# A hybrid attention trunk on one core: tiles of SBUF moved to multiples of 1 and 2 KB

## The chip, the core and the metric

The program runs on one core of a Trainium2 chip, as one launch. The metric is the device time of one execution in microseconds (us); the median of three executions stands for a kernel.

A core has five engines with their own instruction streams: TensorE (PE; the loads of its stationary operand are listed apart, as PEld), VectorE (DVE), ScalarE (ACT), GpSimd (POOL) and SyncE (SP, which here issues all DMA). They share SBUF, 128 partitions of on-chip memory. A tile takes the same bytes of each partition, so its place is one number, its offset in bytes from the start of a partition.

## What is computed

One decoder layer on x of 2048 rows by 1024 columns, in float32, then a last normalization. Cut to what matters:

```python
h = rmsnorm(x, norm_attn)
proj = h @ w_in                              # 1024 x 2700
o_A = stick_breaking(...)                    # 4 heads, all earlier keys
o_B = native_sparse(...)                     # compressed, selected and window branches
o_C = differential(...)                      # 4 heads, two softmax maps each
o_D = sliding_window(...)                    # window 128, sinks
x = x + (concat(norm(o_A), norm(o_B), o_C, norm(o_D)) * g_mix) @ w_out
u = relu(rmsnorm(x, norm_mlp) @ w_up)        # 1024 x 4096
x = x + (u * u) @ w_down                     # 4096 x 1024
return rmsnorm(x, norm_final)
```

## The kernel before

**Stages.** The rows are worked in four chunks of 512. Stages P0 to P3 project a chunk (w_in), stages M0 to M3 do for a chunk what follows the attention: w_out, w_up, w_down and the last normalization. The attention of groups A, C, D and B (loops over 128 queries) runs between them and beside them. A planner in Python, with costs per instruction, decides while the program is written which stream gives PE its next matmul; dense matmuls fill in where a score or value matmul would have to wait. The order on each engine is fixed then. M3 is the last stage, and all attention is over when it runs.

**Dense matmuls in three products.** A float32 operand is split into a rounded part (hi) and the rest (lo), both of type fp32r, and a product is hi*hi + lo*hi + hi*lo, summed in PSUM. PE streams one operand (moving, up to 512 columns) past another (stationary, 128 columns). In a row of the profile, `pdM<-T_hi,w_lo` has the moving operand first and the stationary one second.

- The normalized chunk lies transposed in `T_hi` and `T_lo` (128 x 8 x 512). For w_up and most of w_in it is the moving operand, 512 columns wide, with 128 columns of `w_hi` or `w_lo` stationary (lines 529 and 606).
- For w_down the weight is the moving operand, 512 columns wide, and `u_hi` or `u_lo` (the squared activations) is stationary (line 647).
- For w_out and the value columns of w_in the weight moves, 256 or 268 columns wide, and T is stationary (lines 556 and 591). At the start of each w_up stage T moves in halves of 256 columns (line 634).
- Scores move a key tile `kst`, up to 512 columns (lines 988, 1092).

**The way of a weight.** `load_weights` (line 366) issues the DMA of 512 KB into one of two `raw` tiles; `split_weights` (line 380) writes `w_hi` on ACT and `w_lo` on DVE or POOL into one of three pairs, and gives `raw` back; `weights` (line 398) hands the pair to the matmuls. The order of the weights is that of `weight_specs` (line 325).

**The last normalization.** In the last step of each M stage, for each of four blocks of 128 rows, DVE multiplies by the root mean square and by `last_gain` (lines 657 to 665), and SP stores the rows. `last_gain` is a tile of its own, 4 KB of each partition, loaded once when M0 is written (line 576).

**Where tiles lie.** A pool's tiles follow one another in the order in which they are first made, each place rounded up to 32 bytes; pools stand in the order const, at, dn. The first 16,512 bytes are the program's own. Offsets in bytes, and what is left when they are divided by 1024 and by 128:

| tile | offset of the first buffer | mod 1024 | mod 128 |
|---|---|---|---|
| ident (const) | 16,512 | 128 | 0 |
| row, qst, kst, v, PT, oS, on, scr (at) | row 34,496, kst 71,360 | 704 | 64 |
| small tiles of the attention and pc (at) | 118,464 to 124,063 | any | any |
| T_hi, T_lo, acc, nx (dn) | 124,064 / 140,448 / 156,832 / 173,216 | 160 | 32 |
| small tiles of the norms (dn) | 181,408 to 181,631 | any | any |
| raw, w_hi, w_lo, u_lo, u_hi, r (dn) | 181,632 / 189,824 / 202,112 / 214,400 / 220,544 / 226,688 | 384 | 0 |

Buffers of these tiles are 1, 2, 4, 8 or 16 KB, so every buffer of a tile has the same remainder by 1024. The last tile ends at 228,736 of 229,376 bytes.

Of the kernel before, what the change touches and what calls it, by code (L numbers as in the profile page):

```python
# [9 lines left out]
F32 = mybir.dt.float32  # L10
F32R = mybir.dt.float32r
# [8 lines left out]
D = 1024  # L20
# [11 lines left out]
QB, RB, PB, WB = 4, 7, 3, 3  # L32
PD, ZB, TB = 3, 2, 2
GROUPS = "ACDB"
OFF = S - 128
UO = 2 * (NT - 1)
UW = UO + 32
# [29 lines left out]
def dap(t, off, dims):  # L67
    return bass.AP(tensor=t.tensor, offset=t.offset + off, ap=dims)
# [128 lines left out]
class Trunk:  # L197
# [4 lines left out]
    def __init__(self, ctx, tc, args):  # L202
        self.tc, self.nc = tc, tc.nc
        self.__dict__.update(args)
        nc = self.nc
        self.plan = Plan()
        self.A = Engine(self.plan, "A", nc.scalar, cost_act)
        self.V = Engine(self.plan, "V", nc.vector, cost_dve)
        self.G = Engine(self.plan, "G", nc.gpsimd, cost_pool)
        self.const = ctx.enter_context(tc.tile_pool(name="const", bufs=1))  # L210
        self.dram = ctx.enter_context(tc.tile_pool(name="scratch", bufs=1, space=DRAM))
        self.psum = ctx.enter_context(tc.tile_pool(name="psum", bufs=1, space=PSUM))
        self.at = ctx.enter_context(tc.tile_pool(name="at", bufs=1))
        self.dn = ctx.enter_context(tc.tile_pool(name="dn", bufs=1))
        self.T = (self.dn.tile([128, KD, 512], F32R, name="T_hi", bufs=1),
                  self.dn.tile([128, KD, 512], F32R, name="T_lo", bufs=1))
        self.Tw, self.Tr = [0.0] * 4, [0.0] * 4
        self.filled, self.used, self.fill = [0] * 4, [0] * 4, 0
        self.source, self.added, self.gain = [], {}, {}
        nc.scalar.preload_act_table_set("natural_log_exp_and_others")  # L220
        self.res = {"row": Res(RB), "kst": Res(3), "v": Res(2), "qst": Res(QB), "PT": Res(PB), "w": Res(WB),
                    "raw": Res(2), "nx": Res(2), "acc": Res(4), "oS": Res(3), "pc": Res(1), "unit": Res(UNITS)}
        self.constants()
        self.scratch()
        self.rawq, self.wq = [], []
        self.mix_n = [0] * NT
        self.stored = {}
        self.vq, self.fq = [], []
        self.kq = {}
        self.over, self.pa = set(), "A0"  # L230
        self.compress_due = self.compressed = 0


    def tile(self, pool, shape, dt, name, bufs, tag=None):
        t = pool.tile(shape, dt, name=name, tag=tag or name, bufs=bufs)
        self.plan.new(tag or name, bufs, t.tensor.name)
        return t
# [61 lines left out]

    def constants(self):  # L300
        V, G, const = self.V, self.G, self.const
        self.ident = const.tile([128, 128], F32, name="ident")
        G.memset(self.ident, 1.0)
        G.affine_select(self.ident, self.ident, [[-1, 128]], OP.is_equal, 0.0, base=0, channel_multiplier=1)
        self.mhalf = const.tile([128, 1], F32, name="mhalf")
        G.memset(self.mhalf, -0.5)
        self.qsc = const.tile([128, 6], F32, name="qsc")
        self.qs_col = {}
        for j in range(2):
            for n, (g, sl, dd) in enumerate((("B", SL_NSA, 64), ("C", SL_DIFF, 32), ("D", SL_SWA, 64))):  # L310
                col = n * 2 + j
                self.qs_col[f"q{g}{j}"] = col
                for hh in range(2):
                    V.memset(self.qsc[64 * hh:64 * hh + 64, col:col + 1], -(dd ** -0.5) / sl[2 * j + hh])
# [10 lines left out]
    def weight_specs(self):  # L325
        def w_in(cols, k0, kn):
            wd = sum(w for _, w in cols)
            parts, o = [], 0
            for c0, w in cols:
                def place(t, o=o, w=w):  # L330
                    return t[:, :kn * wd].rearrange("p (k w) -> p k w", k=kn)[:, :, o:o + w]

                parts.append((place, dap(self.w_in, k0 * 128 * IN_COLS + c0,
                                         [[IN_COLS, 128], [128 * IN_COLS, kn], [1, w]])))
                o += w
            return parts

        def up(ft):
            return [(lambda t: t.rearrange("p (k w) -> p k w", k=KD),
                     dap(self.w_up, ft * 128, [[FF, 128], [128 * FF, KD], [1, 128]]))]  # L340

        for kind, c in self.phases:
            if kind == "P":
                for m in ORDER[c > 0]:
                    if m in MT:
                        yield kind, c, w_in(MT[m], 0, KD)
                    else:
                        kn = WMAX // sum(w for _, w in NG[m])
                        for k0 in range(0, KD, kn):
                            yield kind, c, w_in(NG[m], k0, min(kn, KD - k0))  # L350
            else:
                for d in range(4):
                    for kk in range(2):
                        yield kind, c, [(lambda t: t.rearrange("p (k w) -> p k w", k=4),
                                         dap(self.w_out, kk * 512 * D + d * 256, [[D, 128], [128 * D, 4], [1, 256]]))]
                yield kind, c, up(0)
                yield kind, c, up(1)
                for fc in range(FF // 128 // FC):
                    if FC * fc + 2 < FF // 128:
                        yield kind, c, up(FC * fc + 2)  # L360
                    for f in range(FC):
                        yield kind, c, [(lambda t: t, dap(self.w_down, (fc * FC + f) * 128 * D, [[D, 128], [1, D]]))]
                    if FC * fc + 3 < FF // 128:
                        yield kind, c, up(FC * fc + 3)

    def load_weights(self):
        for kind, c, parts in self.weight_specs():
# [12 lines left out]
    def split_weights(self):  # L380
        j = 0
        while True:
            while not self.rawq:
                if "raw" in self.over:
                    return
                yield None
            yield from self.res["w"].take()
            kind, c, raw, n = self.rawq.pop(0)
            hi = self.tile(self.dn, [128, WMAX], F32R, "w_hi", WB)
# [179 lines left out]
    def mlp(self, c):  # L569
# [2 lines left out]
        self.ph = f"M{c}"  # L572
        V, A = self.V, self.A
        acc = []
        if c == 0:
            self.last_gain = self.const.tile([128, D], F32, name="last_gain")
            self.ld(self.last_gain, dap(self.norm_final, 0, [[0, 128], [1, D]]))
        yield from self.res["acc"].take(4)
        for i in range(4):
            a = self.acc_tile()  # L580
# [56 lines left out]
        for fc in range(FF // 128 // FC):  # L637
# [4 lines left out]
            for i in range(4):  # L642
# [14 lines left out]
                if last:  # L657
                    V.tensor_tensor(ss[:, 0:1], ss[:, 0:1], ss[:, 1:2], OP.add)
                    r = self.rstd(dn, ss[:, 0:1], D, "nt")
                    for d in range(2):  # L660
                        o = acc[i][:, d * 512:d * 512 + 512]
                        V.scalar_tensor_tensor(o, o, r[:, 0:1], self.last_gain[:, d * 512:d * 512 + 512], op0=OP.mult,
                                               op1=OP.mult)
                        self.st(dap(self.out, (c * 512 + i * 128) * D + d * 512, [[D, 128], [1, 512]]), o)
                    self.res["acc"].give()
            if FC * fc + 3 < FF // 128:
                yield from up(FC * fc + 3)
            if fc == FF // 128 // FC - 2:
# [6 lines left out]
    def attention_constants(self):  # L675
# [21 lines left out]
        G.affine_select(mask, mask, [[-1, 128]], OP.is_gt, -BIG, base=0, channel_multiplier=1)  # L697
        self.maskr = const.tile([128, 128], F32R, name="maskr")
        V.tensor_copy(self.maskr, mask)
        self.identr = const.tile([128, 128], F32R, name="identr")  # L700
        V.tensor_copy(self.identr, self.ident)

        self.neglam = const.tile([128, 1], F32, name="neglam")
        dl = []
        for a_, b_, nm in ((self.diff_lq1, self.diff_lk1, "l1"), (self.diff_lq2, self.diff_lk2, "l2")):
            u = self.row_tile()[:, :64].rearrange("p (a b) -> p a b", a=2)
            self.ld(u[:, 0, :], dap(a_, 0, [[0, 128], [1, 32]]))
            self.ld(u[:, 1, :], dap(b_, 0, [[0, 128], [1, 32]]))
            s_ = const.tile([128, 1], F32, name="lams_" + nm)
            V.tensor_tensor_reduce(u[:, 0, :], u[:, 0, :], u[:, 1, :], 1.0, 0.0, OP.mult, OP.add, s_)  # L710
            A.activation(s_, s_, AF.Exp)
            dl.append(s_)
        V.tensor_tensor(self.neglam, dl[1], dl[0], OP.subtract)
        V.tensor_scalar(self.neglam, self.neglam, -LAM_INIT, None, op0=OP.add)

        self.snk = const.tile([128, 4], F32, name="snk")
        self.ld(self.snk, dap(self.sinks, 0, [[0, 128], [1, 4]]))
        self.nsnk = const.tile([128, 4], F32, name="nsnk")
        V.tensor_scalar(self.nsnk, self.snk, -1.0, None, op0=OP.mult)

        self.kcs = const.tile([128, 128], F32R, name="kcs")
# [846 lines left out]
```

## Time and profile before

| | us |
|---|---|
| median of three executions | 3219.77 |
| lowest and highest of them | 3219.07, 3225.04 |
| the profiled execution, its own time | 3224.61 |
| its span, first to last instruction | 3222.9 |

The profile is of one execution, and its durations belong to the 3224.61 us. A matmul's listed duration (about 0.39 us at 512 columns) holds its way through the array; the next one starts before it ends. What a stream of matmuls costs is therefore the step from one start to the next, which the timeline shows to 0.01 us; over 25 steps it is known to better than 1 ns.

### The profile page before, as it was taken

The numbers are of one execution on the slowest core, as the hardware profiler recorded it, in microseconds if no ns is written. First come the engines' busy times: TensorE is split into PE (matmuls) and PEld (weight loads), VectorE is DVE, ScalarE is ACT, GpSimd is POOL, SyncE is SP. The second block draws the span as 40 slices with busy tenths as digits, with TensorE's granted clock in tenths as the row PEclk, the third lists the DMA queues.
The fourth block names the chain that finished last, engine by engine and source line by source line (L and its number), as shares of the span: only waits on it lengthen the run. The fifth ranks groups of instructions, "written<-read, shape, count | busy, mean of one in ns | idle before, by whom it ended". The sixth has DMA issues, their size and how long they took to land.

```text
span 3222.9 us, 51242 instructions
## 1 busy us (share of the span) xinstructions
PE 3128.8 (97%) x19152; PEld 2510.3 (78%) x19152; DVE 2063.7 (64%) x4278; ACT 1776.0 (55%) x3459; POOL 714.2 (22%) x479
## 2 busy tenths in 40 slices
PE   7999999999999999999999999999999999999998
PEld 6887877878877777778877677778777777888886
DVE  4774668645668877666658887777655554545545
ACT  4764667545667755555657775565555543333333
POOL 3042312323212122232211122233212112310000
PEclk9999999999999999999999999999999999999999
DMA  7777555664133343364232333444522222423332
GB/s 213 193 193 206 160 160 148 191 176 134 57 97 87 100 110 105 97 164 121 61 100 68 99 95 88 110 117 134 141 63 83 65 61 74 149 81 97 92 98 85
DMA packets 456649, 376.53 MB, mean 117 GB/s; under 512 B 127056, under 2 KB 405712, under 8 KB 454736
## 3 DMA queue, kind: packets, MB, share of 16 engines
q1 hardware_dynamic: 456400, 373.26, 42.0%
q8 instruction: 151, 2.47, 0.3%
q14 instruction: 98, 0.80, 0.1%
HBM read 319.59 MB, written 53.58 MB: 116 GB/s over the span
## 4 chain that ended last, share of the span: by engine, by line
PE 77%; DVE 9%; ACT 5%; DMA 4%; issue 2%; SPq 1%; POOL 1%; DVEq 0%; POOLq 0%; ACTq 0%
PE pdM L290 43%; PE pdP L290 11%; DVE row L116 7%; PE tB L294 4%; PE oB L290 4%; PE zB L290 4%; ACT row L116 4%; PE oC L290 2%; PE zC L290 2%; PE tC L294 2%; SPq L246 1%; PE oA L290 1%; DVE acc L116 1%; PE tA L294 1%; PE zA L290 1%
## 5 line engine op out<-in xcount | busy, mean ns | idle before, releaser
L116 POOL TENSOR_TENSOR w_lo<-raw,w_hi 128x1024 fp32r<-128x1024 f32 (+1 forms) x188 | 469.4, 2501 | 1248.9 <-ACT w_hi L116 1105.4
L116 ACT ACTIVATE w_hi<-raw 128x1024 fp32r<-128x1024 f32 (+2 forms) x376 | 388.2, 1047 | 499.4 <-PE pdM L290 309.5
L116 DVE TENSOR_TENSOR acc<-acc,pdM 128x512 f32<-128x512 f32 (+1 forms) x576 | 370.3, 654 | 193.5 <-PE pdM L290 182.0
L290 PE MATMUL pdM<-T_lo,w_hi 128*128 128x512 f32 (+1 forms) x1088 | 419.6, 386 | 4.4 <-POOL T_lo L116 4.4
L290 PE MATMUL pdM<-T_hi,w_hi 128*128 128x512 f32 (+1 forms) x1088 | 419.5, 387 | 3.8 <-DVE nx L116 2.2
L290 PE MATMUL pdM<-T_hi,w_lo 128*128 128x512 f32 (+1 forms) x1088 | 420.8, 387 | 0.0
L290 PE MATMUL pdM<-w_hi,u_hi 128*128 128x512 f32 x1024 | 405.5, 403 | 11.6 <-DVE acc L116 8.4
L290 PE MATMUL pdM<-w_hi,u_lo 128*128 128x512 f32 x1024 | 405.2, 396 | 3.9 <-DVE u_lo L116 3.9
L290 PE MATMUL pdM<-w_lo,u_hi 128*128 128x512 f32 x1024 | 404.7, 396 | 0.0
L116 DVE TENSOR_TENSOR w_lo<-raw,w_hi 128x1024 fp32r<-128x1024 f32 (+1 forms) x188 | 241.2, 1290 | 214.5 <-ACT w_hi L116 206.0
L116 ACT ACTIVATE row<-row 128x1024 f32<-128x1024 f32 (+7 forms) x292 | 229.0, 801 | 118.5 <-DVE row L116 115.8
L290 PEld LDWEIGHTS pdM<-T_lo,w_hi 128*128 128x128 f32 x1088 | 206.5, 190 | 45.9 <-POOL T_lo L116 4.9
L290 PEld LDWEIGHTS pdM<-T_hi,w_hi 128*128 128x128 f32 x1088 | 206.0, 190 | 45.3 <-DVE nx L116 2.5
L116 ACT ACTIVATE PT<-tB 128x512 f32<-128x512 f32 (+1 forms) x260 | 135.9, 532 | 189.4 <-PE tB L294 186.7
L290 PEld LDWEIGHTS pdM<-T_hi,w_lo 128*128 128x128 f32 x1088 | 206.4, 190 | 42.1 <-issue 1.0
L290 PEld LDWEIGHTS pdM<-w_hi,u_hi 128*128 128x128 f32 x1024 | 193.2, 189 | 58.0 <-DVE acc L116 13.2
L290 PEld LDWEIGHTS pdM<-w_hi,u_lo 128*128 128x128 f32 x1024 | 193.7, 189 | 42.7 <-DVE u_lo L116 5.3
L290 PEld LDWEIGHTS pdM<-w_lo,u_hi 128*128 128x128 f32 x1024 | 193.6, 189 | 41.4 <-issue 1.2
L116 ACT ACTIVATE row<-row,c_mn 128x1024 f32<-128x1024 f32 (+4 forms) x192 | 171.6, 896 | 85.6 <-DVE c_mn L116 84.4
L290 PE MATMUL pdP<-T_hi,w_lo 128*128 128x512 f32 x480 | 194.1, 404 | 3.7 <-DVE w_lo L116 3.7
L290 PE MATMUL pdP<-T_lo,w_hi 128*128 128x512 f32 x480 | 193.4, 403 | 0.0
L290 PE MATMUL pdP<-T_hi,w_hi 128*128 128x512 f32 x480 | 192.7, 401 | 0.0
(209 smaller groups left out, 6604.8 us busy)
## 6 DMA issues: line engine op xcount, KB each, us to landing
raw<-in_w_up_dram SPq DMA_DIRECT2D x128, 512.0 KB, 4.1
raw<-in_w_down_dram SPq DMA_DIRECT2D x128, 512.0 KB, 3.6
raw<-in_w_in_dram SPq DMA_DIRECT2D x72, 512.0 KB, 4.9
acc<-in_x_dram SPq DMA_DIRECT2D x32, 512.0 KB, 4.3
raw<-in_w_out_dram SPq DMA_DIRECT2D x32, 512.0 KB, 4.4
qst<-qk_qA SPq DMA_DIRECT2D x64, 128.0 KB, 3.5
qst<-qk_qC SPq DMA_DIRECT2D x128, 64.0 KB, 2.6
qst<-qk_qD SPq DMA_DIRECT2D x64, 128.0 KB, 3.4
```

The source lines that it names most:

```text
L116: return f(*a, **k)
L246: self.nc.sync.dma_start(dst, src)
L290: self.nc.tensor.matmul(out, a, b, start=start, stop=stop, **k)
L294: self.nc.tensor.transpose(out, a, self.ident[:a.shape[0], :a.shape[0]])
```

## The change

Five edits. (1) A tile `pad` of 816 floats is made first in the pool const. (2) A pool `sm` is opened ahead of at and dn, and takes every tile of theirs whose elements per partition are no multiple of 256. (3) `last_gain` is gone: each M stage ends its list of weights with norm_final, which is loaded into a `raw` tile, handed on unsplit, and given back after the fourth block of rows. (4) `ident` is gone: the identity is built in a row tile, copied to `identr`, and `ident` is `identr` read as float32. (5) Two pairs of small constants share a tile.

```diff
+PAD = 816
...
+        self.sm = ctx.enter_context(tc.tile_pool(name="sm", bufs=1))
         self.at = ctx.enter_context(tc.tile_pool(name="at", bufs=1))
...
+        self.const.tile([128, PAD], F32, name="pad")
         self.constants()
...
     def tile(self, pool, shape, dt, name, bufs, tag=None):
+
+        if pool in (self.at, self.dn) and math.prod(shape[1:]) % 256:
+            pool = self.sm
...
-        self.ident = const.tile([128, 128], F32, name="ident")
-        G.memset(self.ident, 1.0)
-        G.affine_select(self.ident, self.ident, [[-1, 128]], OP.is_equal, 0.0, base=0, channel_multiplier=1)
+        one = self.row_tile()[:, :128]
+        G.memset(one, 1.0)
+        G.affine_select(one, one, [[-1, 128]], OP.is_equal, 0.0, base=0, channel_multiplier=1)
+        self.identr = const.tile([128, 128], F32R, name="identr")
+        V.tensor_copy(self.identr, one)
+        self.ident = self.identr.bitcast(F32)
...
                     if FC * fc + 3 < FF // 128:
                         yield kind, c, up(FC * fc + 3)
+                yield "G", c, [(lambda t: t, dap(self.norm_final, 0, [[0, 128], [1, D]]))]
...
+            if self.rawq[0][0] == "G":
+                self.wq.append(self.rawq.pop(0)[2])
+                continue
             yield from self.res["w"].take()
...
-        if c == 0:
-            self.last_gain = self.const.tile([128, D], F32, name="last_gain")
-            self.ld(self.last_gain, dap(self.norm_final, 0, [[0, 128], [1, D]]))
...
+                    if i == 0:
+                        gain, = yield from self.weights()
                     for d in range(2):
                         o = acc[i][:, d * 512:d * 512 + 512]
-                        V.scalar_tensor_tensor(o, o, r[:, 0:1], self.last_gain[:, d * 512:d * 512 + 512], op0=OP.mult,
+                        V.scalar_tensor_tensor(o, o, r[:, 0:1], gain[:, d * 512:d * 512 + 512], op0=OP.mult,
                                                op1=OP.mult)
                         self.st(dap(self.out, (c * 512 + i * 128) * D + d * 512, [[D, 128], [1, 512]]), o)
                     self.res["acc"].give()
+                    if i == 3:
+                        self.res["raw"].give()
...
-        dl = []
-        for a_, b_, nm in ((self.diff_lq1, self.diff_lk1, "l1"), (self.diff_lq2, self.diff_lk2, "l2")):
+        lams = const.tile([128, 2], F32, name="lams")
+        dl = [lams[:, 0:1], lams[:, 1:2]]
+        for a_, b_, s_ in ((self.diff_lq1, self.diff_lk1, dl[0]), (self.diff_lq2, self.diff_lk2, dl[1])):
...
-        self.snk = const.tile([128, 4], F32, name="snk")
+        snk = const.tile([128, 8], F32, name="snk")
+        self.snk, self.nsnk = snk[:, 0:4], snk[:, 4:8]
```

## Rows read from the trace of the kernel before

**Rows 1.** The page: busy time and instructions of each engine; the chain by engine.
```profile
PE 3128.8 (97%) x19152; PEld 2510.3 (78%) x19152; DVE 2063.7 (64%) x4278; ACT 1776.0 (55%) x3459; POOL 714.2 (22%) x479
...
PE 77%; DVE 9%; ACT 5%; DMA 4%; issue 2%; SPq 1%; POOL 1%; DVEq 0%; POOLq 0%; ACTq 0%
```

**Rows 2.** Windows: stretch, length, busy of PE, PEld, DVE, ACT, POOL; clock, DMA.
```profile
1700.00:2000.00 300.00, 287.40 (x1695) 216.20 (x1692) 245.28 (x316) 215.38 (x340) 56.62 (x26) 0.98 0.32 86
...
2900.00:3180.00 280.00, 280.00 (x1217) 227.99 (x1216) 143.33 (x180) 94.92 (x124) 0.00 (x0) 1.00 0.32 96
```

**Rows 3.** The chain in order of time, 2700 to 3223 us: start, length, what.
```profile
2863.62 345.87 PE pdM L290 x1523
```

**Rows 4.** Groups of instructions on PE, by form: count, busy us, mean ns.
```profile
L290 PE MATMUL pdM<-w_hi,u_hi 128*128 128x512 f32 x1024 | 405.5, 403 | 11.6 <-DVE acc L116 8.4 <-ACT u_hi L116 2.3 <-ACT r L116 0.8
...
L290 PE MATMUL pdM<-T_hi,w_lo 128*128 128x512 f32 x960 | 383.0, 399 | 0.0
...
L290 PE MATMUL pdP<-T_hi,w_lo 128*128 128x512 f32 x480 | 194.1, 404 | 3.7 <-DVE w_lo L116 3.7
...
L290 PE MATMUL pdM<-w_hi,T_hi 128*128 128x256 f32 x512 | 145.9, 287 | 0.0
...
L290 PE MATMUL zB<-kst,qst 128*128 128x512 f32 x328 | 106.6, 416 | 0.8 <-DVE b_mw L116 0.7
```

**Rows 5.** Timeline of PE in M3, w_up: first and last of 26.
```profile
3172.94 0.40 PE L290 MATMUL pdM<-T_hi,w_hi 128*128 128x512 f32 x1
...
3178.77 0.40 PE L290 MATMUL pdM<-T_lo,w_hi 128*128 128x512 f32 x1
```

**Rows 6.** Timeline of PE in M3, w_down: first and last of 27.
```profile
3188.94 0.39 PE L290 MATMUL pdM<-w_hi,u_hi 128*128 128x512 f32 x1
...
3194.83 0.39 PE L290 MATMUL pdM<-w_lo,u_hi 128*128 128x512 f32 x1
```

**Rows 7.** Timeline of PE in M3, w_out, 256 columns: first and last of 10.
```profile
2809.83 0.28 PE L290 MATMUL pdM<-w_hi,T_lo 128*128 128x256 f32 x1
...
2810.89 0.28 PE L290 MATMUL pdM<-w_hi,T_lo 128*128 128x256 f32 x1
```

**Rows 8.** Timeline of PE in M3, w_up in halves: first and last of 11.
```profile
2864.78 0.28 PE L290 MATMUL pdM<-T_lo,w_hi 128*128 128x256 f32 x1
...
2865.94 0.28 PE L290 MATMUL pdM<-T_hi,w_lo 128*128 128x256 f32 x1
```

**Rows 9.** Timeline of PE, eight transposes in one piece.
```profile
2794.39 1.03 PE L294 MATMUL pdM<-ident,nx 128*128 128x128 f32 x8
```

**Rows 10.** The tile ident: durations in ns, least, median, most.
```profile
L294 PE MATMUL pdM<-ident,nx x256: 270/273/477, 728.4 to 2859.4; 128*128 128x128 f32 x128
```

**Rows 11.** Groups of instructions on ACT, by form: count, busy us, mean ns.
```profile
L116 ACT ACTIVATE w_hi<-raw 128x1024 fp32r<-128x1024 f32 x364 | 378.6, 1055 | 495.2 <-PE pdM L290 309.5 <-DMA raw<-in_w_down_dram 72.0 <-issue 37.0
...
L116 ACT ACTIVATE nx<-acc 128x1024 f32<-128x1024 f32 x32 | 33.8, 1055 | 26.2 <-DMA acc<-in_x_dram 17.7 <-DVE acc L116 6.0 <-POOL T_lo L116 2.3
```

**Rows 12.** The tile last_gain: its DMA, from issue to landing.
```profile
DMA to landing us min/median/max: 7.0/7.0/7.0
```

**Rows 13.** Timeline of DVE where M2 ends and M3 has begun.
```profile
2807.22 1.41 DVE L116 SCALAR_TENSOR_TENSOR acc<-acc,nt_rs,last_gain 128x512 f32<-128x512 f32 x2 [0.20 <-POOL nt_rs L116]
...
2810.53 1.23 DVE L116 TENSOR_TENSOR w_lo<-raw,w_hi 128x1024 fp32r<-128x1024 f32 x1 [1.57 <-ACT w_hi L116]
```

**Rows 14.** The page's DMA issues: count, KB each, us to landing.
```profile
raw<-in_w_out_dram SPq DMA_DIRECT2D x32, 512.0 KB, 4.4
```

**Rows 15.** Timeline of DVE at the end of M3.
```profile
3195.86 2.35 DVE L116 TENSOR_TENSOR w_lo<-raw,w_hi 128x1024 fp32r<-128x1024 f32 x2
...
3213.10 1.40 DVE L116 SCALAR_TENSOR_TENSOR acc<-acc,nt_rs,last_gain 128x512 f32<-128x512 f32 x2
```

**Rows 16.** Timeline of all engines at the start.
```profile
2.41 0.56 DVE L116 CAST identr<-ident 128x128 fp32r<-128x128 f32 x1
...
11.34 1.97 PE L294 MATMUL pdP<-ident,acc 128*128 128x128 f32 x8 [11.34 <-DVE nt_ms L116]
```

More of the change, by code (lines that the diff above doesn't have):

```diff
@@ L699, in attention_constants @@
         V.tensor_copy(self.maskr, mask)
-        self.identr = const.tile([128, 128], F32R, name="identr")
-        V.tensor_copy(self.identr, self.ident)
         self.neglam = const.tile([128, 1], F32, name="neglam")
-        dl = []
-        for a_, b_, nm in ((self.diff_lq1, self.diff_lk1, "l1"), (self.diff_lq2, self.diff_lk2, "l2")):
+        lams = const.tile([128, 2], F32, name="lams")
+        dl = [lams[:, 0:1], lams[:, 1:2]]
+        for a_, b_, s_ in ((self.diff_lq1, self.diff_lk1, dl[0]), (self.diff_lq2, self.diff_lk2, dl[1])):
             u = self.row_tile()[:, :64].rearrange("p (a b) -> p a b", a=2)
@@ L708, in attention_constants @@
             self.ld(u[:, 1, :], dap(b_, 0, [[0, 128], [1, 32]]))
-            s_ = const.tile([128, 1], F32, name="lams_" + nm)
             V.tensor_tensor_reduce(u[:, 0, :], u[:, 0, :], u[:, 1, :], 1.0, 0.0, OP.mult, OP.add, s_)
             A.activation(s_, s_, AF.Exp)
-            dl.append(s_)
         V.tensor_tensor(self.neglam, dl[1], dl[0], OP.subtract)
         V.tensor_scalar(self.neglam, self.neglam, -LAM_INIT, None, op0=OP.add)
-        self.snk = const.tile([128, 4], F32, name="snk")
+        snk = const.tile([128, 8], F32, name="snk")
+        self.snk, self.nsnk = snk[:, 0:4], snk[:, 4:8]
         self.ld(self.snk, dap(self.sinks, 0, [[0, 128], [1, 4]]))
-        self.nsnk = const.tile([128, 4], F32, name="nsnk")
         V.tensor_scalar(self.nsnk, self.snk, -1.0, None, op0=OP.mult)
```

## The prediction

> **What bounds the kernel now.** I read the page first. PE is busy for 3128.8 of 3222.9 us and holds 77% of the chain that ended last [rows 1], so PE bounds the kernel unless it is busy only because its matmuls are listed long. The windows settle that: from 2900 to 3180 us PE is never idle, at a granted clock of 1.00 (the 2.4 GHz level), and starts 1217 matmuls in 280 us; from 1700 to 2000, in the attention, it is idle for 4% while DVE is busy for 82% [rows 2]. The chain by time says the same of M3: 345.87 us of it, to 11 us before the end, are one unbroken piece of PE [rows 3]. So a nanosecond off the step of a dense matmul shortens the kernel, and the next question is what sets that step.
>
> The timeline gives it. In w_up, where T moves, 25 steps take 5.83 us: 233.2 ns each [rows 5]. In w_down, where w moves, 26 steps take 5.89 us: 226.5 ns [rows 6]. Both move 512 columns of the same type past 128 fresh stationary columns, at the same clock; 512 columns at 2.4 GHz are 213.3 ns. So T's stream loses 19.9 ns and w's 13.2. The difference, 6.7 ns, is the time of 16 columns, or 64 bytes of a partition. What else separates them is where they lie: T's slices start 32 bytes past a multiple of 128, w's on a multiple of 128, both off any multiple of 256. The trace doesn't prove that this is the cause, but the layout is what this change alters.
>
> **The change part by part.**
>
> *The offsets after.* Const starts at 16,512 bytes, gains 3,264 for pad and loses 4,096 (last_gain), 512 (ident) and two places of 32 bytes: it ends at 33,088. The pool sm then takes 5,600 bytes of small attention tiles and 224 of small norm tiles: 38,912, which is 19 times 2,048. From there come only tiles of whole kilobytes. T_hi lands at 122,880, raw at 180,224, w_hi at 188,416, u_lo at 212,992, all multiples of 2,048; only oS, on and scr are at multiples of 1,024. It fits: r ends at 227,328.
>
> *T as the moving operand.* 3 x 960 matmuls in the M stages and 3 x 480 in the P stages, 4320 in all ([rows 4], where one of each three equal groups stands). Bounds: no gain at all, or down to the bare 213.3 ns, 4320 x 19.9 = 86 us. Between ends so far apart I take the nearest row: after the change T starts on a multiple of 128, as w does today, so it gets w's step: 4320 x 6.7 = 28.8 us.
>
> *w as the moving operand, 512 wide.* 3 x 1024 = 3072 matmuls [rows 4]. w already starts on a multiple of 128 and goes to one of 2,048. No operand of the trace lies so, and nothing says what the 13.2 ns are. Bounds: a gain of 3072 x 13.2 = 40.6 us; a loss if the common offset hurts, by the only loss the trace shows, 6.7 ns: 20.5 us. I take 0, as for T: no nearer row than w itself.
>
> *The 256-wide matmuls.* w moving past a stationary T steps at 1.06 / 9 = 117.8 ns [rows 7]; T moving past w at 1.16 / 10 = 116.0 [rows 8]; the columns alone need 106.7. Here the operand 32 bytes off is no slower, which speaks against the address (see the rivals). 3 x 512 and 3 x 256 matmuls: 0 taken, at most 2304 x 11.1 = 25.6 us. The scores move kst from a multiple of 64, and no long run of them stands in the trace: 0 to 5 us (776 x 6.7; 328 of them in rows 4), 0 taken.
>
> The rule of the Trainium skill that speaks against the change stands in "TensorE: Matmul & The Clock Gate", section "Back-to-back issue gap": a warm matmul follows the one ahead after its columns at 2.4 GHz plus about 2.5 ns, with no term for an address. By it both steps would be an estimated 215.8 ns and moving T would be worth 0 instead of 28.8 us. The trace disagrees with it on the step, 233.2 and 226.5 ns.
>
> *The other engines.* ACT takes 1055 ns for 1024 elements both from raw (a multiple of 128) and from acc (32 off) [rows 11]. So I give ACT and DVE nothing for their offsets. No row shows a DMA into a tile on a multiple of 256 bytes; whatever it gained could come only out of PE's idle time, 3222.9 - 3128.8 = 94 us in all and mostly not DMA's [rows 1], so I take 0.
>
> *norm_final through raw.* One DMA early in the program goes, four come, one at the end of each M stage, and each holds one of two raw tiles until the stage's last multiplication by the gain. At the end of M3 it is hidden: its raw tile is free when the last weights are split, at 3195.86 + 2.35 = 3198.2, a gain lands 7.0 us after its issue [rows 12], at 3205.2, and the first product with it starts at 3213.10 [rows 15]. That cover is 7.9 us; beyond it each us late is a us at the end, because DVE closes the kernel. At the three other ends the next stage's w_out tiles come through one raw tile meanwhile. At the end of M2 the third w_out tile can be loaded only when the second is split, and the fourth only when the last gain product is done, at 2807.22 + 1.41 = 2808.6; with 4.4 us to land [rows 14], 1.06 on ACT and 1.23 on DVE it is ready at 2815.3, against 2811.8 now [rows 13]. PE reaches it after the 96 matmuls of the first quarter, some 2 us sooner. SP's queue keeps behind that load the loads of acc, which are not wanted before; in DVE's queue nothing waits that hadn't. At M0 and M1 attention fills such gaps. Bounds: 0, and three times the whole way 4.4 + 1.06 + 1.23, 20 us. I take 3 us.
>
> *ident from identr.* A copy of 0.56 us that ran anyway now stands ahead of the first transpose. It ended at 2.97 us and PE starts at 11.34 [rows 16]: hidden by 8 us of normalizing; without that cover it would cost its 0.56 us. Merged constants, pad and sm issue nothing.
>
> *The sum.* Not all of the 28.8 us arrives: in the attention PE already waits for 4% [rows 2], and a faster PE waits more on DVE. I pass on nine tenths: 26 us, less 3 for raw, 23 us. The profiled execution would take 3224.6 - 23 = 3201.6; it lies 4.8 us above the median shown, so the median comes to 3219.8 - 23 = 3197 us. I call 0.2%, 6.4 us, the least that a measurement tells from no change; the three runs before spread over 6.0.
>
> **The rivals.**
>
> *All of the loss goes.* If a stream loses whatever a start off 1 or 2 KB costs, T and w both end near their columns. The nearest row for what then remains is the transposes: eight take 1.03 us, the last of them 0.27 [rows 9, 10], so the step is 0.76 / 7 = 108.6 ns, 1.9 above the 106.7 of the 256 columns that the planner counts. At 215.2 ns T gains 18.0 x 4320 = 77.8 us, w 11.3 x 3072 = 34.7, and the 256-wide ones at 108.6 gain 9.2 x 2304 = 21.2: 133.7, nine tenths 120, less 3: 3103 us. With every bound in full, 3219.8 - 86 - 40.6 - 25.6 = 3068. For it: w's offset isn't a multiple of 256 either, so w's 13.2 ns may be the rest of the same loss. Against: they may as well be the price of exchanging the stationary operand each time, which no address touches.
>
> *The address isn't it.* T and w differ also in who is stationary and in what came before. For it: at 256 columns T moves no slower than w [rows 7, 8]. Then the steps stay 233.2 and 226.5 and only raw is left: 3223 us, at worst 3240. The skill's rule, quoted above, would have this too.
>
> *One common offset hurts.* After the change every slice that moves and every slice loaded beside it starts at the same remainder of 512. If the two reads then meet in the same place of SBUF, w's step rises to T's of today, 3072 x 6.7 = 20.5 us, and T's stays: 3240 us, slower. It decides as soon as the mean step in M3's dense stretch is above today's 280 / 1217 = 230.1 ns [rows 2]. Against: u and w, both 384 past a multiple of 1,024 today, are the faster pair.
>
> **How the numbers follow.** Forecast 0.45, all of the loss 0.25, not the address 0.18, common offset 0.12. The forecast's own range, from two thirds of T's gain with 8 us lost at raw to all of it with kst's, is 3187 to 3209. The range for 8 in 10 leaves out the common offset and half of the no-change case, and takes the other case down to half-way between its price and its bound: 3085 to 3223. Faster by over 0.2%: the forecast and all of the loss, 0.70. Within 0.2%: most of not the address, 0.15. Slower: the common offset and the worst of raw, 0.15.
>
> **What would show it.** In M3's w_up the step of T: 226.5 right, 233.2 the address isn't it, near 215 all of the loss. In w_down the step of w: 226.5 right. At the end of M2, w_lo of the fourth w_out tile some 3 us later after M2's last gain product than now, and PE idle for at most a few us. In M3's tail no DVE wait on the gain. I am wrong if w's step moves, in either direction, or if T's steps fall and the attention stretches grow by as much.

## The result: 0.6% faster, for a cause that the forecast had half

The changed kernel takes 3202.74 us, the median of six runs (3196.0 to 3204.39), against 3219.7 for the kernel before beside it (six runs, 3217.99 to 3225.04): a ratio of 0.9939, 95% interval 0.9926 to 0.9952. On another chip it was 0.9933 (0.9919 to 0.9946). So it is faster by 17 to 21 us; the forecast was 23.

The profiled executions differ by more, 3224.61 and 3198.36 us, and the clock is part of that. By the trace's record of the granted clock, the execution of before ran 58.0 us at 1.2 GHz, apart from its tail, in 11 stretches, and this one 34.1 us in 7; the difference is worth up to 12 us. The second profiled execution of the changed kernel, with 47.8 us at that level, took 3206.63. Verdicts below go by medians and ratios, and the traces serve for steps and waits.

The page of the changed kernel answers [rows 1], PE's busy time first, then the chain by engine:

```profile
PE 3104.2 (97%) x19152; PEld 2510.6 (79%) x19152; DVE 2054.8 (64%) x4278; ACT 1777.8 (56%) x3459; POOL 714.6 (22%) x479
...
PE 75%; DVE 10%; ACT 7%; DMA 4%; issue 3%; SPq 1%; POOL 1%; DVEq 0%; POOLq 0%; ACTq 0%
```

The windows of the same stages, M3 shifted by its 21 us, answer [rows 2]: 1237 matmuls in 280 us of dense work in place of 1217, 226.4 ns each and not 230.1.

```profile
1700.00:2000.00 300.00, 284.23 (x1668) 214.95 (x1667) 242.45 (x321) 207.23 (x329) 59.86 (x26) 0.99 0.31 85
2879.00:3159.00 280.00, 280.00 (x1237) 231.86 (x1236) 145.01 (x181) 96.48 (x127) 0.00 (x0) 1.00 0.33 98
```

The chain by time answers [rows 3]: the same 1523 matmuls without a break take 5.25 us less. In the timeline of PE, T's step in w_up is (3153.44 - 3147.78) / 25 = 226.4 ns, where it was 233.2 [rows 5]; w's in w_down is 5.89 / 26 = 226.5, as before [rows 6].

```profile
2843.15 340.62 PE pdM L296 x1523
```

```profile
3147.78 0.39 PE L296 MATMUL pdM<-T_hi,w_hi 128*128 128x512 f32 x1
...
3153.44 0.39 PE L296 MATMUL pdM<-T_lo,w_hi 128*128 128x512 f32 x1
...
3162.74 0.39 PE L296 MATMUL pdM<-w_hi,u_hi 128*128 128x512 f32 x1
...
3168.63 0.39 PE L296 MATMUL pdM<-w_lo,u_hi 128*128 128x512 f32 x1
```

At 256 columns both streams became slower, which no part of the sum had. Nine steps in w_out take 1.08 us, 120.0 ns each, against 117.8 [rows 7]; ten in w_up's halves take 1.19 us, 119.0 against 116.0 [rows 8].

```profile
2788.42 0.28 PE L296 MATMUL pdM<-w_hi,T_lo 128*128 128x256 f32 x1
...
2789.50 0.28 PE L296 MATMUL pdM<-w_hi,T_hi 128*128 128x256 f32 x1
...
2843.49 0.28 PE L296 MATMUL pdM<-T_hi,w_hi 128*128 128x256 f32 x1
...
2844.68 0.28 PE L296 MATMUL pdM<-T_lo,w_hi 128*128 128x256 f32 x1
```

Over all long runs of one kind in the two traces, from start to start: T at 512 columns 233.3 and 227.4 ns, w at 512 227.8 and 227.4, w past T at 256 118.2 and 119.7, T past w at 256 116.8 and 119.5.

These are steps of long runs, and two thirds of T's 512-wide matmuls stand among the first ten of their run, ahead of the next matmul of another kind. There the gain is smaller. Mean step of T at 512 columns by its place in the run:

| step of the run | before, ns | after, ns |
|---|---|---|
| second to fourth | 232.4 | 230.5 |
| fifth to tenth | 233.3 | 228.1 |
| from the eleventh | 233.3 | 226.7 |

The means leave out steps over 0.3 us and those at 1.2 GHz. One run of seven, as an example: its six steps take 1.40 us before and 1.39 after.

```profile
1200.70 0.39 PE L290 MATMUL pdM<-T_hi,w_lo 128*128 128x512 f32 x1
...
1202.10 0.39 PE L290 MATMUL pdM<-T_hi,w_lo 128*128 128x512 f32 x1
```

```profile
1192.15 0.39 PE L296 MATMUL pdM<-T_hi,w_lo 128*128 128x512 f32 x1
...
1193.54 0.39 PE L296 MATMUL pdM<-T_hi,w_lo 128*128 128x512 f32 x1
```

Over all 4320 of them, from each start to the next, with waits over 0.15 us left out and time at 1.2 GHz counted half, they take 1031.1 us before and 1012.2 after: 4.4 ns less each, 18.9 us.

norm_final's raw tile did what was described, and PE hardly felt it. At the end of M2 the last gain product ends at 2786.61 + 1.42 = 2788.0, and w_lo of the fourth w_out tile at 2797.68 + 1.22 = 2798.9, 10.9 us later. Before it was 4.5 us (w_lo at 2811.95 to 2813.2 after 2808.6; the row of [rows 13] that I took for the fourth tile's is the third's). PE's waits from there to the first w_up tiles sum to 5.4 us, against 5.9 before, and none is for a weight. In all of M0 to M3 PE's waits for a weight sum to 0 us here, 2.2 in the second trace of this kernel and 0.2 before. At the end of M3, SP issues the gain's load at 3171.59, such loads land after 3.8 us, and the first product that needs it starts at 3187.38 without a wait: the cover is 12 us, not 7.9 [rows 12, 15]. DVE in its order of time:

```profile
2786.61 1.42 DVE L117 SCALAR_TENSOR_TENSOR acc<-acc,nt_rs,raw 128x512 f32<-128x512 f32 x2 [0.73 <-POOL nt_rs L117]
...
2797.68 1.22 DVE L117 TENSOR_TENSOR w_lo<-raw,w_hi 128x1024 fp32r<-128x1024 f32 x1 [0.19 <-ACT w_hi L117]
...
3187.38 1.40 DVE L117 SCALAR_TENSOR_TENSOR acc<-acc,nt_rs,raw 128x512 f32<-128x512 f32 x2
```

### The profile page after: what moved, and what is told of

The parts are those of the page before. It is cut to its first block, busy times and chain, and to the rows that moved or that the text cites. A ratio compares the mean times of both kernels' runs of the same rounds, so it can differ in the third digit from the quotient of the medians.

```text
span 3196.6 us, 51283 instructions
## 1 busy us (share of the span) xinstructions
PE 3104.2 (97%) x19152; PEld 2510.6 (79%) x19152; DVE 2054.8 (64%) x4278; ACT 1777.8 (56%) x3459; POOL 714.6 (22%) x479
## 4 chain that ended last, share of the span: by engine, by line
PE 75%; DVE 10%; ACT 7%; DMA 4%; issue 3%; SPq 1%; POOL 1%; DVEq 0%; POOLq 0%; ACTq 0%
PE pdM L296 41%; PE pdP L296 12%; DVE row L117 7%; ACT row L117 4%; PE tB L300 4%; PE oB L296 4%; PE zB L296 4%; PE oC L296 2%; PE zC L296 2%; PE tC L300 2%; SPq L252 1%; DVE acc L117 1%; ACT w_hi L117 1%; DMA raw<-in_w_in_dram 1%; PE oA L296 1%
```

## Experiments

Theory A, the forecast's: a moving slice that starts off a multiple of 128 bytes loses some 6 ns in 512 columns. Against it stood that tiles must lie at multiples of 1 or 2 KB (D), that the two operands' starts act together (B), and that the gain comes from the order of work or from norm_final (C). The first runs put E in A's place: the step goes by the difference of the two starts. The later ones added F: where a tile starts sets the cost of a DMA into it.

### Streams of matmuls (e1, e5)

```
for (w, m, s): 32 x (24 x in e5)  matmul(z[:, :w], st[:, s/4 + 128*(j%8):+128], mv[:, m/4 + 512*(j%8):+w])
```

> This kernel leaves the whole computation out: it runs streams of 32 dependent-free matmuls of constant data, each stream with one width (512 or 256 columns), one start of the moving slice and one start of the stationary slice in a partition's bytes, with a fresh stationary slice for each matmul or the same one throughout, and writes zeros and sums of constants to the output. Theory A (the start of the moving slice within 128 bytes sets the step): at 512 columns 227 ns for starts at 0, 128, 256, 384 and 512, 233 ns for 16, 32, 48, 96 and 160 bytes past a multiple of 2 KB, 64 undecided; the start of the stationary slice changes nothing. Rival B (the stationary slice's start, or the two together, set it): 227 ns for all moving starts, a change where the stationary one moves. Rival C (neither; what separated the two streams before was their content or their neighbours in time): 227 ns throughout. For 256 columns the two kernels' traces give 116 to 118 ns before and 119 to 120 after: if the common offset costs these, the stream with both starts at 0 steps at 119 to 120 and those with 160 and 384 bytes at 116 to 118. With the same stationary slice throughout, 213 to 216 ns if the 13 ns that are left over the columns are the price of exchanging it, 227 if not.

The timeline of PE has one line a stream; the name gives columns and the moving start (m), its last number, the stationary start, is cut off. It is 0 in the first eight lines shown and in those of 256 columns, 32 in the line at 148.63 and 384 in that at 155.92.

```profile
30.34 7.42 PE L50 MATMUL c512m0s<-mv,st 128*128 128x512 f32 x32
37.59 7.57 PE L50 MATMUL c512m16s<-mv,st 128*128 128x512 f32 x32
45.00 7.63 PE L50 MATMUL c512m32s<-mv,st 128*128 128x512 f32 x32
52.48 7.62 PE L50 MATMUL c512m48s<-mv,st 128*128 128x512 f32 x32
...
74.75 7.63 PE L50 MATMUL c512m128s<-mv,st 128*128 128x512 f32 x32
82.21 7.65 PE L50 MATMUL c512m160s<-mv,st 128*128 128x512 f32 x32
89.70 7.43 PE L50 MATMUL c512m256s<-mv,st 128*128 128x512 f32 x32
96.97 7.62 PE L50 MATMUL c512m384s<-mv,st 128*128 128x512 f32 x32
...
148.63 7.44 PE L50 MATMUL c512m32s<-mv,st 128*128 128x512 f32 x32
155.92 7.63 PE L50 MATMUL c512m160s<-mv,st 128*128 128x512 f32 x32
163.38 14.91 PE L50 MATMUL c512m384s<-mv,st 128*128 128x512 f32 x64
...
207.63 3.99 PE L50 MATMUL c256m0s<-mv,st 128*128 128x256 f32 x32
211.45 3.97 PE L50 MATMUL c256m16s<-mv,st 128*128 128x256 f32 x32
```

From start to start over 32 matmuls: both at 0, 7.25 / 32 = 226.6 ns; moving at 32, 233.8; at 128, 233.1, which ends theory A; at 256, 227.2. Both at 32: 7.29 / 32 = 227.8, as fast as both at 0. At 160 against 384, which is T against w in the kernel before: 233.1. So 512 columns go fast where the two slices start at the same place within 256 bytes, which w and u did before and T and w did not. At 256 columns the common start gives 3.82 / 32 = 119.4, one of the slowest. The streams with the same stationary slice throughout load it anew each time (1440 loads for 1440 matmuls), so they say nothing on the 13 ns that remain.

> Streams alone again, the computation left out: the moving slice at a multiple of 2 KB throughout, the stationary slice 0 to 252 bytes past one, in steps of 4, at 512 and at 256 columns. New theory E, from the first streams (226.7 ns where both slices start at the same place within 256 bytes, wherever that is, 229 to 234 elsewhere): the step depends on the difference of the two starts alone, and the least step at 512 columns is 226.7, near a difference of 0 to 16 bytes; at 256 columns common starts are the worst, 119.9, and 64 bytes the best seen, 113.3. Theory A (the moving slice's own start within 128 bytes) is refuted by the first streams and would give one step throughout. If some difference gives 512 columns less than 226.7, say 220, a better layout than both kernels' exists, worth 7392 x 6.7 = 49 us.

At 512 columns no difference gave less than 226.7 ns: of 64, seven gave it (0, 120, 144, 156, 204, 228 and 252 bytes), and most of the others lie between 229 and 236. Away from 0 a step isn't fixed by the difference alone: at 16 bytes it was 226.7 in the first streams and 233.3 in the second. At 256 columns the common start gave 120.0, and 64, 76, 88 and 180 bytes 113.3. The kernel before fits to some 0.3 ns: its differences are 224 bytes where T moves (stream 233.2 and 116.8, kernel 233.3 and 116.8) and 32 where w moves past T at 256 (118.2 in both).

### Parts of the change (e2, e3, e4, e6)

In all four the order of PE's matmuls is that of the kernel before, but for e3, which has the changed kernel's; the two differ at some 5800 of 19,152 places, and only the edit of norm_final brings that.

```
e2  before  + self.dn.tile([128, 24], F32, name="pad1")   # ahead of T_hi
            + self.dn.tile([128, 8], F32, name="pad2")    # ahead of raw
e3  before  + the lines of norm_final through raw, last_gain removed
e4  after   - the lines of norm_final through raw;  -PAD = 816  +PAD = 48
e6  e4      + dn.tile([128, 8], ...) ahead of T_hi, + dn.tile([128, 56], ...) behind T_lo
```

> The kernel before with two unused tiles, 96 bytes ahead of T_hi and 32 ahead of raw, and nothing else: T starts on a multiple of 128 bytes (256 past one of 1 KB), raw, w and u 512 past one of 1 KB; no tile goes to a pool of its own, norm_final is loaded as before. Theory A (a moving slice that starts off a multiple of 128 bytes costs 6 ns in 512 columns): T's step 227 ns, 4320 x 5.9 = 25.7 us less, of which nine tenths, 23 us, show: 3197 us. Rival D (tiles must start at multiples of 1 or 2 KB): 3220, T's step 233. Rival C (the gain has come from the order of work or from norm_final): 3220. If the 256-wide matmuls lose only by a common offset, they stay at 116 to 118 ns here.

3208.92 us against 3221.63, ratio 0.9958 (0.9946 to 0.9971). T's step was 227.4 ns, so two pads do all that the change does to the matmuls, the 256-wide ones included (119.7 and 119.8, as they now share a start). But 13 us came, not 23. Over all matmuls, summed as above, this kernel's steps are 15 us shorter than those of the kernel before, so nearly all of it arrived; the changed kernel's 17 to 21 us and the 23 of e4 (below) need something else besides.

> The kernel before with norm_final through a raw tile alone; T still starts 32 bytes past a multiple of 128. My forecast's term for it: 3 us slower, 3223, with T's step at 233 ns. Rival C (part of the gain is norm_final's): 3220 or less, down to 3203 if it is all of it.

3221.25 us, ratio 1.0001 (0.9993 to 1.001): norm_final and the new order together bring and cost nothing net. The runs had a mean granted clock of 0.993 against 0.991, worth up to 6 us, so a cost of that size may hide behind a better clock.

> The changed kernel with norm_final in a tile of its own again (large tiles at multiples of 1 KB, since 2 KB don't fit with it). If the raw tile that norm_final holds costs 3 us, 3200 us; if it costs nothing, 3203; if multiples of 2 KB matter beside those of 1 KB, above 3206.

3200.23 us, ratio 0.9928 (0.9914 to 0.9941): within the spread of the changed kernel's 0.9933 and 0.9939. What the raw tile costs is between 0 and some 3 us; the runs don't resolve it. Multiples of 2 KB do nothing that those of 1 KB don't.

> The changed kernel with norm_final in a tile of its own and large tiles at multiples of 1 KB (3200 us when run), with T alone put 32 bytes past such a multiple and all tiles behind it 256 past: T against w as in the kernel before, the order of work and all else as in the changed one. Theory E: T's step back at 233.3 ns, 25.7 us more in the matmuls and 4 less at 256 columns, nine tenths of 21: 3200 + 19 = 3219. If the order of work, with fewer dips of the clock, carries some 6 us of the gain beside T: 3213 to 3216. If multiples of 1 KB matter for themselves (rival D), also above 3200, since the tiles behind T are at 256.

3218.1 us, ratio 0.9981 (0.9972 to 0.999). T's step is back at 233.3, and the piece of 1523 matmuls is back as well; 3.4 us at 1.2 GHz fall into it, so 1.7 of the 347.3 are the clock's:

```profile
2851.64 347.30 PE pdM L298 x1523
```

Against e4, T's start is worth 0.0053 of 3223, 17 us. And with T as slow as before, the kernel is still 6 us faster than before, in the same order of work: a second effect of the layout (with up to 4 us of it in the granted clock, 0.9913 against 0.9901 on the mean).

### The same layout, shifted (e7, e10, beside e9)

```
-PAD = 816        e7: +PAD = 824 (all large tiles 32 bytes on)    e10: +PAD = 832 (64 bytes on)
```

> The changed kernel with 32 bytes more in pad, so that every large tile starts 32 bytes past a multiple of 1 or 2 KB, with their differences as they were. Theory E (only the difference of the two starts counts): T and w both at 227.4 ns, 3203 us. Theory A (each slice must start at a multiple of 128 bytes): 233.3 ns for both, 3203 + 0.9 x 7392 x 5.9 = 3242. Rival D (multiples of 1 or 2 KB): the same 3242.

> The changed kernel once more, on the same chip as the two that follow: 0.994 of the kernel before, as measured first.

> The changed kernel with every large tile 64 bytes past a multiple of 1 or 2 KB, differences of starts as they were; matmul steps at 227.4 ns, as with 32. With 32 bytes the time was 0.9974 of before in place of 0.994, 11 us lost with no matmul slower. Theory F: a start at a multiple of 64 costs DMA less than one at 32: 0.994 to 0.996, 3202 to 3210. If only 1 or 2 KB help: 0.9974, as with 32. If the 11 us were the chip's or the clock's: 0.994.

The steps held as E says, 227.4 ns for T and for w in both, so an own alignment of either slice is not needed. The times did not hold: e7 3215.28 us, ratio 0.9974 (0.9963 to 0.9985); e10 3211.09, 0.9961 (0.9948 to 0.9974); the changed kernel on e10's chip 3202.27, 0.9933. So 32 or 64 bytes cost 9 to 13 us with no matmul slower: the piece of 1523 takes 340.62 us in e10 as in the changed kernel. The waits of PE say where most of it goes (us in total, times, longest); e10 first, then the changed kernel:

```profile
PE zA L296 <- ACT row L117: 5.5, 7, 1.8
PE zC L296 <- DMA row<-in_cmp_w_k_dram: 4.5, 3, 2.4
...
PE zB L296 <- DMA qst<-qk_qB: 3.8, 4, 2.1
```

```profile
PE zA L296 <- ACT row L117: 3.9, 6, 1.6
...
PE zC L296 <- DMA row<-in_cmp_w_k_dram: 2.6, 2, 1.5
...
PE zB L296 <- DMA qst<-qk_qB: 2.4, 4, 1.2
```

All rows of that view add up to 90.3 us in e10 and 91.9 in e7, 80.6 and 83.2 in the two traces of the changed kernel, 82.3 in the kernel before: with T's step cut and the large tiles off a multiple of 256, PE waits 8 to 10 us more. The queue of the transfers, its packets, megabytes and share of the 16 engines, in the kernel before, e10 and the changed one:

```profile
q1 hardware_dynamic: 456400, 373.26, 42.0%
```

```profile
q1 hardware_dynamic: 456832, 374.83, 42.2%
```

```profile
q1 hardware_dynamic: 456832, 374.83, 41.4%
```

### Loads by themselves (e8)

```
for (piece, o): 12 x  dma_start(t[:, o/4 + 1024*j : +1024], 512 KB in pieces of 256, 512 or 4096 bytes)
```

> This kernel leaves the whole computation out: on one queue it issues groups of twelve loads of 512 KB each, in pieces of 256, 512 or 4096 bytes, into tiles that start 0, 32, 64, 96, 128, 256, 512 or 1024 bytes past a multiple of 2 KB, and writes zeros. Theory F (where a tile starts sets what a DMA packet into it costs, which is the rest of the change's gain): packets of 256 and 512 bytes take some 3 to 8% longer at 32 and 96 than at 0, less at 64 and 128, as the full kernels' packets did (256 bytes: 19.2 ns mean at multiples of 1 KB, 20.5 at 704, 20.7 at 32; 512 bytes: 30.1, 30.9, 31.3), and groups take as much longer. Rival G (the packets' times in the full kernels come from what else runs): no difference between the starts.

The issues of this kernel by tile, p the piece and o the start (count, KB each, median us from issue to landing):

```profile
p256o0x<-in_x_dram SPq DMA_DIRECT2D x12, 512.0 KB, 6.3
p256o32x<-in_x_dram SPq DMA_DIRECT2D x12, 512.0 KB, 7.6
...
p256o256x<-in_x_dram SPq DMA_DIRECT2D x12, 512.0 KB, 6.3
...
p512o0x<-in_w_up_dram SPq DMA_DIRECT2D x12, 512.0 KB, 6.1
p512o32x<-in_w_up_dram SPq DMA_DIRECT2D x12, 512.0 KB, 7.3
p512o64x<-in_w_up_dram SPq DMA_DIRECT2D x12, 512.0 KB, 7.3
p512o128x<-in_w_up_dram SPq DMA_DIRECT2D x12, 512.0 KB, 7.3
p512o256x<-in_w_up_dram SPq DMA_DIRECT2D x12, 512.0 KB, 6.0
...
p4096o0x<-in_w_down_dram SPq DMA_DIRECT2D x12, 512.0 KB, 8.5
p4096o32x<-in_w_down_dram SPq DMA_DIRECT2D x12, 512.0 KB, 9.2
```

A load in pieces of 256 or 512 bytes takes 20% longer, when the queue is full, wherever its tile starts off a multiple of 256, and 32, 64 and 128 are alike. With pieces of 4 KB the groups differ without an order (7.9 to 9.2). The Trainium skill's page "DMA: Bandwidth & Descriptors", section "How a descriptor splits into AXI transactions", says that a transaction reads up to 256 bytes and has to begin at a 256-byte boundary, and that what is fetched ahead of an unaligned start costs beats too. The page speaks of reading; here it is the writing into SBUF that starts off the boundary. The boundary of 256 agrees with the rows (6.3 and 6.0 us at 256); by its count of beats a start at 128 would be dearer than one at 32, which the rows don't show.

### The layout alone, and a better one (e11, e12)

```
e11 before + pool sm and the line in tile() that uses it;  +PAD = 32
e12 after: w_hi, w_lo = tile([128, WMAX + 64])[:, o:];  o = 48 for w_out, vA, vC;  16 for up(0), up(1);  else 0
```

> The kernel before with the change's layout alone: small tiles in a pool of their own and 128 bytes of padding, so that every large tile starts 512 past a multiple of 1 KB; ident, last_gain and the merged constants stay as before. If layout is all there is (T's step with 13 us, starts at multiples of 512 with some 7): 0.993 to 0.994, 3199 to 3201. If the new order of work that the other edits bring carries the 7 us: 0.996, 3208, as with the two pads.

3201.88 us, ratio 0.9934 (0.9922 to 0.9947), the same as the changed kernel on the same chip, with 512 past a multiple of 1 KB for all large tiles. The layout alone gives the whole net change; multiples of 1 KB aren't needed either. Against e2, whose T and w step alike, it is some 8 us faster; its granted clock, 0.9918 on the mean against 0.9899 before, is worth up to 6 of them.

> The changed kernel with the split weights alone moved inside their tiles, which are 256 bytes longer: the weights of w_out, vA and vC, which move 256 columns past T, start 192 bytes past a multiple of 256, those of the first two w_up tiles, past which T moves 256 columns at a time, 64 past; so the stationary slice starts 64 bytes behind the moving one, where the streams showed 113.3 ns for 256 columns against 119.9 for a common start. All 512-wide matmuls keep the common start, all DMA goes to multiples of 256. Theory E: 2304 x 6.4 + 384 x 6.2 = 17 us less in the matmuls, of which three quarters show: 3189 us, 0.989 of the kernel before. If the streams' locking at 113.3 ns doesn't hold between the real kernel's neighbours: 118 ns and 3200 us. If the order of work or the clock takes it back: 3202.

3198.62 us, ratio 0.9914 (0.9901 to 0.9928), the lowest ratio, but its interval overlaps that of the changed kernel and that of e4. In w_out, 18 steps take 2.04 us, 113.3 ns; over all long runs w past T stepped at 115.1 and T past w at 114.2. By these steps 2304 x 4.6 + 384 x 5.3 = 12.6 us would be saved, not 17; summed over all 256-wide matmuls the trace has 8 us less than the changed kernel's. The time is 0.0019 of 3223 lower, 6 us, with an interval of about 0 to 12: a gain at the end isn't shown clear of noise.

```profile
2790.97 0.28 PE L296 MATMUL pdM<-w_hi,T_hi 128*128 128x256 f32 x1
...
2793.01 0.28 PE L296 MATMUL pdM<-w_lo,T_hi 128*128 128x256 f32 x1
```

## Why the forecast was right, step by step

The time fell at 3203 where 3197 stood, on the forecast's own case: T's step shortened, and the gain arrived. That the sum came so close is in part luck. T's term was 10 us too large, and the transfers, taken as 0, and norm_final, taken as a loss, made up for most of it.

**T's step** was right in long runs: it got w's, 5.9 ns less and not 6.7. The price was mis-sized. 25 steps from the middle of a long run stood for all 4320 matmuls, and most of those stand in shorter runs, where the gain is smaller. Over all of them it is 4.3 to 4.4 ns and 18 to 19 us, where 28.8 stood (18.9 in the changed kernel's trace, 18.4 between e4 and e6). The reason given, multiples of 128, was wrong (e1, e7): it is enough that T and w start at the same place within 256 bytes. It came true because the change puts both on such a place.

**w at 512 columns** was right near 0: 0.4 ns in long runs, and 0.4 to 3.6 us less over all of them (e2 least, the changed kernel most). w and u had a common start all along.

**The 256-wide matmuls** were taken as 0 and lose 2.0 to 3.6 us, between kernels with the same order of work. The rows that I held against the address [rows 7, 8] were the sign of it: at 256 columns a common start is the slower one. In all PE's steps give back 15 us in e2, 17 in e11, 17 between e6 and e4, and 19 between e3 and the changed kernel.

**DMA** was taken as 0, and is the other mis-sized term. "No row shows a DMA into a tile on a multiple of 256 bytes" was so; the bound of 94 us of idle PE held too, but some of that idle time does hang on transfers. In the kernel before raw starts 128 bytes off a multiple of 256 and the attention's tiles 64 off. Starts on a multiple go with 6 us less beside a slow T (e6) and 9 to 13 beside a fast one (e7, e10); with intervals of 3 us either way for the first and 6 for the others, that a fast T raises their price isn't shown.

**Nine tenths passed on** holds as far as the runs tell: 13 of 15 us in e2 (9 to 17 by its interval), and 17 of 17 between e6 and e4 (12 to 22). Only where the large tiles start 32 or 64 bytes off do 8 and 12 of some 19 us arrive (e7, e10), and there PE's waits are longer. So 17 for the steps and 6 for the transfers make 23 us; 21 (e11) and 23 (e4) were measured for the layout, 17 to 21 for the whole change, and 26 - 3 = 23 forecast.

**The clock** had no term. A thousandth of it is worth up to 3.2 us. In e2 the mean granted clock is that of the kernel before (0.9910 and 0.9911), so T's gain stands without it. In e6 it is 0.0012 above the kernel before, in e11 and e3 0.002, in the changed kernel on e11's chip 0.0035. How much of what is put down to the transfers, and of the work that norm_final may cost, passes through the clock, and what raises it, no run separates.

**norm_final through raw**, 3 us: the fourth w_out tile comes later, as described, and PE waits for none of it at the end of M2. Net 0 was measured (e3), with at most some 3 us open (e4); before the clock it may cost more. The unbroken piece of [rows 3] ends 13.4 us before the end, not 11; nothing in the sum hangs on it.

The rivals: "the address isn't it" falls with e1, where nothing but the start differs; no stream came near the 215.8 ns that the prediction quotes from the Trainium skill, page "TensorE: Matmul & The Clock Gate", section "Back-to-back issue gap". The page gives that formula for an isolated matmul and says that it counts too much for a stream at large widths; the streams here all lie above it, at 226.7 ns and more. "All of the loss goes" falls with e5: no start gave less than 226.7 ns at 512 columns, and what the remaining 13 ns are stays open. "One common offset hurts" had the effect and its sign wrong at 512 columns, and right at 256. Why a common start makes 512 columns faster and 256 slower wasn't settled by any run.

## What to carry over

Before tuning a layout, read the step from start to start for each pair of moving and stationary tile, and compare the two starts within 256 bytes; a padded tile or two then does for the matmuls what a rearrangement would. Price the gain over short runs too: 5.9 ns in long runs of T were 4.3 on the mean. Put what DMA fills in small pieces on multiples of 256 bytes, also where the DMA queue looks half idle. Time saved on the bound engine arrived nearly whole in e2 and between e6 and e4, and about half in e7 and e10, where the waits grew, so price the feeding with it. And compare the granted clock of the runs before a few us are put down to a cause.

## What the runs showed of the hardware

Many steps of fp32r matmuls settle at whole 16 columns of 2.4 GHz over the columns moved: 226.7 ns is 544, 233.3 is 560, 120.0 is 288 and 113.3 is 272 (others settle between, at 230.0 or 116.7); a common start gave 512 + 32 and 256 + 32, and 64 bytes between the starts 256 + 16. In the full kernel the step of T comes down to that only after some ten matmuls of its kind. ACT's split didn't care where its tiles start: w_hi from raw takes 1055 ns before [rows 11] and 1056 after. And the spread of one kernel's runs goes with the clock: the six first runs of the changed kernel go from 3196.0 us at a mean granted clock of 0.995 to 3203.73 at 0.992 and 3204.39 at 0.993.
